# The second block's experts: runs of 1792 columns, a branch on the row count for TensorE, and half of the third matrix unsplit

## Chip, core and metric

One core of one Trainium2 chip. The metric is the device time of one execution in microseconds; TensorE, VectorE (DVE), ScalarE (ACT), GpSimd (POOL) and SyncE (SP, which issues most loads) run side by side and wait for one another by semaphores.

## What is computed

256 tokens of width 1024 pass a first block (latent attention beside a recurrent group, then 32 small experts) and a second block of two layers. The second layer of the second block ends in eight large experts, and that is where the change lies:

```python
def swiglu(h, w1, w3, w2):
    return (jax.nn.silu(h @ w1) * (h @ w3)) @ w2

def moe_swiglu(h, w_router, w1, w3, w2):
    B, S, D = h.shape
    t = h.reshape(B * S, D)
    logits = (t @ w_router).astype(jnp.float32)
    top_vals, top_idx = lax.top_k(logits, TOP_K)
    top_w = jax.nn.softmax(top_vals, axis=-1)
    gates = jnp.sum(jax.nn.one_hot(top_idx, N_EXPERTS_2, dtype=jnp.float32) * top_w[..., None],
                    axis=1).astype(h.dtype)
    out = jnp.zeros_like(t)
    for e in range(N_EXPERTS_2):
        out = out + gates[:, e:e + 1] * swiglu(t, w1[e], w3[e], w2[e])
    return out.reshape(B, S, D)
```

Each token goes to two of the eight experts. `w1` and `w3` of an expert are 1024 x 3584 and `w2` is 3584 x 1024, in fp32: 44 MB per expert, 352 MB in all. After the experts come a layer norm and a gated addition, which end the kernel.

## The kernel before

Products whose operands are wide are made of split operands: `K.split` (line 88) makes `hi`, a copy in the reduced format fp32r by ScalarE, and `lo`, the rest, by VectorE (or GpSimd, if asked), and `K.mm3` (line 110) adds hi x hi, hi x lo and lo x hi on TensorE, three matmuls for one. In line numbers of the profile ScalarE's half of a split is L99, VectorE's is L100, and the three matmuls are L113, L114 and L115.

The experts are in `moe` (line 1514). The router's logits give each token two experts; the rank of a token within its expert is its slot, up to 128 slots. `gather` makes the transposed rows of the slots of two experts at a time, split into `xgh` and `xgl`, by products with one-hot matrices (L1574). An expert then goes through `NS` = 7 steps of 512 hidden columns. In a step `half` makes the 512 gate columns and, called again, the 512 up columns: for each it loads two tiles [128, 4, 512] of 1 MB, splits them, and makes 24 matmuls with the slots' rows as the stationary operand and the weights moving. `hidden` (L1603, L1604) makes silu(gate) x up, `turned` transposes it by four transposes (L1610) and splits it, and `down` loads and splits two tiles of `w2` and adds 24 matmuls to two banks of sums. The second product of a step is issued between the products of the next (`second`, a generator). At an expert's end `finish` splits the sums, puts the rows back to their tokens (`back`, L1631) and adds them into `x` with the routing weights (`add`, L1636).

Weights come by SP's queue (L85) through a ring of 6 tiles (`raw`), and the split halves lie in a ring of 4 (`spl`); both rings stay open through all phases of the second block (`stream_pools` in `whole`). In the experts, two or three of eight loads go to other room (`xgh1`, `xgl1`, `xw`). Instructions of an engine run in the order of the program text, except where `K.behind` (line 103) puts some behind a named instruction. PSUM has eight banks of 512 columns.

`past` (L1684, L1685) is a branch of all engines for experts with more than 128 rows; its body isn't run here. A like branch stands in the first block's experts (L993). Those 32 experts (L1074, L1105) use unsplit fp32 weights with 32 slots each, four experts side by side in four groups of 32 columns of the array.

The tail of `mixer` makes `p @ ple_w` for the first token tile (`ple_products`); in the second layer the second tile's product is made in `moe`, while the routes are made.

## Time and profile before

| | us |
|---|---|
| median of 3 runs | 1985.56 |
| lowest and highest | 1983.2, 1987.6 |
| span of the profiled execution | 1980.7 |
| TensorE busy (matmul) | 1845.0 (93%) |
| VectorE busy | 1402.4 (71%) |
| ScalarE busy | 1102.0 (56%) |
| GpSimd busy | 171.9 (9%) |
| read from memory | 543 MB, 275 GB/s over the span |

The busy times are those of one execution, which spanned 1980.7 us from its first to its last instruction. Matmuls overlap their neighbours' latency, so that a matmul's own duration (some 0.39 us for 512 columns) is longer than the distance at which the next one starts; the price of one in a row is that distance. A group's idle time names who ended most of it.

### The profile page before, as it was taken

To read this page: it belongs to the slowest core of one execution; us is meant where nothing else is said; L and a number is where in the kernel's file an instruction comes from. 1 tells how busy PE (TensorE), PEld (TensorE's weight loads), DVE (VectorE), ACT (ScalarE), POOL (GpSimd) and SP (SyncE) were. 2 spreads that over 40 slices of the span, in tenths; PEclk is the share of its full clock that TensorE was granted. 3 is DMA by queue.
4 is the path that set the end of the run, shared out by engine and by line. 5 is a ranking of instruction groups with operands and counts; after the bars stand their busy time and mean duration, and the time that the engine had idled before them with its cause. 6 is when DMAs were issued, how large, how long until landed. Compare 5 with 4: busy or idle time off the path is not lost. (4 is left out here: it accounts for less than half of the span.)

```text
span 1980.7 us, 25915 instructions
## 1 busy us (share of the span) xinstructions
PE 1845.0 (93%) x10327; PEld 1471.6 (74%) x10327; DVE 1402.4 (71%) x1508; ACT 1102.0 (56%) x1223; POOL 171.9 (9%) x249
## 2 busy tenths in 40 slices
PE   7988698877989999888999999999999999999997
PEld 6878464323779999777888887878878778788785
DVE  5675542101886554887889889888888888888986
ACT  6444341101474443555777666776767666677673
POOL 3051210000400000234100000000000000000002
PEclk8989689989999999999999999999999999999998
DMA  7000579999755555444899889999999999899991
GB/s 223 30 1 1 201 288 402 421 421 401 261 165 178 186 186 174 150 149 161 300 377 367 301 327 346 366 363 356 349 334 363 340 371 343 309 365 374 347 373 53
DMA packets 224412, 545.82 MB, mean 276 GB/s; under 512 B 12817, under 2 KB 45724, under 8 KB 211997
## 3 DMA queue, kind: packets, MB, share of 16 engines
q1 hardware_dynamic: 218476, 536.06, 73.2%
q10 hardware_dynamic: 5536, 6.99, 1.1%
q8 instruction: 83, 1.36, 0.3%
q0 software_dynamic: 272, 1.05, 0.2%
q14 instruction: 45, 0.36, 0.1%
HBM read 543.01 MB, written 1.05 MB: 275 GB/s over the span
## 5 line engine op out<-in xcount | busy, mean ns | idle before, releaser
L100 DVE TENSOR_TENSOR wlo<-raw,whi 128x2048 fp32r<-128x2048 f32 (+1 forms) x436 | 804.7, 1881 | 147.2 <-ACT whi L99 146.7
L99 ACT ACTIVATE whi<-raw 128x2048 fp32r<-128x2048 f32 (+1 forms) x460 | 679.2, 1526 | 102.6 <-PE ps L115 68.6
L114 PE MATMUL ps<-wlo,xgh 128*128 128x512 f32 x896 | 358.3, 400 | 5.0 <-PEq L1685 3.8
L113 PE MATMUL ps<-whi,xgh 128*128 128x512 f32 x896 | 354.9, 396 | 0.0
L115 PE MATMUL ps<-whi,xgl 128*128 128x512 f32 x896 | 351.7, 393 | 0.0
L114 PEld LDWEIGHTS ps<-wlo,xgh 128*128 128x128 f32 x896 | 169.0, 189 | 47.1 <-DVE wlo L100 8.8
L113 PEld LDWEIGHTS ps<-whi,xgh 128*128 128x128 f32 x896 | 168.6, 188 | 38.1
L115 PEld LDWEIGHTS ps<-whi,xgl 128*128 128x128 f32 x896 | 169.1, 189 | 35.4
L114 PE MATMUL ps<-wlo,hTh 128*128 128x512 f32 x452 | 180.1, 399 | 2.0 <-DVE wlo L100 2.0
L115 PE MATMUL ps<-whi,hTl 128*128 128x512 f32 x452 | 177.1, 392 | 0.8 <-DVE hTl L100 0.8
L113 PE MATMUL ps<-whi,hTh 128*128 128x512 f32 x452 | 163.9, 392 | 0.2 <-ACT hTh L99 0.2
L114 PE MATMUL ps<-xTl,whi 128*128 128x256 f32 x576 | 161.9, 282 | 1.5 <-DVE xTl L100 1.5
L115 PE MATMUL ps<-xTh,wlo 128*128 128x256 f32 x544 | 153.8, 284 | 3.0 <-DVE wlo L100 2.8
L113 PE MATMUL ps<-xTh,whi 128*128 128x256 f32 x544 | 152.0, 282 | 0.4 <-ACT xTh L99 0.4
L100 POOL TENSOR_TENSOR wlo<-raw,whi 128x512 fp32r<-128x512 f32 (+2 forms) x24 | 41.5, 1758 | 1072.5 <-PE ps L1631 990.4
L99 ACT ACTIVATE hTh<-ps 128x512 fp32r<-128x512 f32 x56 | 33.5, 598 | 148.7 <-PE ps L1610 145.4
L114 PEld LDWEIGHTS ps<-xTl,whi 128*128 128x128 f32 x576 | 108.7, 189 | 3.6 <-DVE xTl L100 2.6
L115 PEld LDWEIGHTS ps<-xTh,wlo 128*128 128x128 f32 x544 | 104.2, 192 | 5.3 <-DVE wlo L100 5.2
L114 PEld LDWEIGHTS ps<-wlo,hTh 128*128 128x128 f32 x452 | 85.1, 188 | 28.9 <-DVE wlo L100 12.4
L113 PEld LDWEIGHTS ps<-xTh,whi 128*128 128x128 f32 x544 | 102.3, 189 | 1.7 <-ACT xTh L99 0.9
L100 DVE TENSOR_TENSOR wlo<-xw,whi 128x2048 fp32r<-128x2048 f32 (+1 forms) x43 | 96.2, 2236 | 5.0 <-ACT whi L99 5.0
L113 PEld LDWEIGHTS ps<-whi,hTh 128*128 128x128 f32 x452 | 85.2, 188 | 18.6 <-ACT hTh L99 0.5
(526 smaller groups left out, 2749.6 us busy)
## 6 DMA issues: line engine op xcount, KB each, us to landing
raw<-in_exp_w_dram SPq DMA_DIRECT2D x280, 1024.0 KB
xw<-in_exp_w_dram SPq DMA_DIRECT2D x40, 1024.0 KB
raw<-in_dense_w_dram SPq DMA_DIRECT2D x33, 1024.0 KB
gu<-in_w_up_dram SPq DMA_DIRECT2D x32, 1024.0 KB
dn<-in_w_down_dram SPq DMA_DIRECT2D x32, 1024.0 KB
gu<-in_w_gate_dram SPq DMA_DIRECT2D x29, 1024.0 KB
raw<-in_w_in_dram SPq DMA_DIRECT2D x19, 1024.0 KB
raw<-in_w_out_dram SPq DMA_DIRECT2D x8, 1024.0 KB
```

The lines of the kernel that those rows point to most:

```text
L99: self.last = [nc.scalar.activation(hi[o], src[o], AF.Copy).ins, (engine or nc.vector).tensor_tensor(lo[o], src[o], hi[o], op=SUB).ins]
L100: (engine or nc.vector).tensor_tensor(lo[o], src[o], hi[o], op=SUB).ins]
L113: mm(out, a[0], b[0], start=first, stop=False)
L114: mm(out, a[0], b[1], start=False, stop=False)
L115: return mm(out, a[1], b[0], start=False, stop=last).ins
```

## The change

- An expert goes through `NS` = 2 runs of 1792 hidden columns. A tile of `w1` or `w3` is 128 rows x 1792 columns (917,504 bytes, 7 KB per partition in one piece); a run's gate columns stand in four banks (`BANKS`), then its up columns.
- After the last tile of gate or up, ScalarE copies the four banks out to SBUF (`evict`). They are transposed by TensorE unhidden, gate and up both (`turn`), four chunks of 128 at a time into two banks; silu and the product with up are made of the transposed values (`turned`).
- The slots are ordered so that rows 0 to 63 of an expert stand at even places, and `g` holds high and low parts in one tile. A register of TensorE holds each expert's row count (`many`), and `arms` makes a branch: over 64 rows, three products as before; else `piece` takes a stationary operand of 64 high and 64 low columns (every second element of 256) and makes two products, with the weights' high and low parts. The sum of both halves is made in `turn`, by an fp32 product with the matrix `both` in place of a transpose, and at the end through the one-hot matrix (`transposed`). Where `cut` is set a product is made in pieces of 256 columns, so that both arms have as many instructions.
- Of the 14 chunks of a run's part of `w2`, seven are split as before (tiles 0 to 3), and seven (tiles 4 to 7) are used as loaded, in unsplit fp32, for few rows with 64 stationary columns, the two halves of the output in two column groups.
- The loop goes by jobs of two tiles: four of gate, four of up, then four of the run before in `w2`; the next job's loads and splits are issued ahead of a job's products.
- `ple_products` of both token tiles stand in the mixer's tail. The rings are closed before and after the experts; theirs have six tiles raw and four split, of 1792 columns. Two tiles are loaded early to the room of the second pair's rows.

Comments were also taken out. Of the diff, what the text speaks of:

```diff
-EX = 60    # loads of the second block's experts before the first pair's rows have been used
+RAW = 6
...
-        for t in range(1 if l else 2):
+        for t in range(NT):
             self.ple_products(t, tuple(z[:, :, t * P:(t + 1) * P] for z in pT))
...
-        E, NS = 8, 7
+        E, NS, HALF = 8, 2, P // 2
+        MS, R = 1792, 7
+        BANKS = ((0, 512), (512, 512), (1024, 512), (1536, 256))
...
+        up_of = lambda n, e, s, k: a[n][0, e, k * P:(k + 1) * P, s * MS:(s + 1) * MS]
+        def down_of(e, s, j):
+            o = s * MS + j // 4 * (MS // 2)
+            rows = a["exp_w2_2"][0, e, o:o + MS // 2, :].rearrange("(p r) d -> p (r d)", r=R)
+            return rows[:, j % 4 * MS:(j % 4 + 1) * MS]
...
+        def arms(e, f):
+            with tc.If(many[e] > HALF) as c:
+                f(False)
+            with c.Else():
+                f(True)
+        def piece(few, rows, w, i, to, first, last, cut):
+            if few:
+                few_rows = rows.rearrange("p i s -> p (i s)")[:, 0::2]
+                n = i.stop - i.start
+                for o in range(0, n, 256 if cut else n):
+                    m = 256 if cut else n
+                    for q in range(2):
+                        mm(to[:, o:o + m], few_rows, w[q][:, i.start + o:i.start + o + m], start=first and o == 0 and q == 0, stop=last and o + m == n and q == 1)
+            else:
+                for q, (a_, b_) in enumerate(((0, 0), (0, 1), (1, 0))):
+                    mm(to, rows[:, a_], w[b_][:, i], start=first and q == 0, stop=last and q == 2)
+        def up(few, e, g, to, k, w):
+            for b, (o, n) in enumerate(BANKS):
+                piece(few, g[:, k, e % 2], w, slice(o, o + n), to[b][:, :n], k == 0, k == KC - 1, b < 2)
+        def down(few, s, hT, acc, j, w):
+            c0, c, cuts = j % 4 * MS, j % 4 * MS, 0
+            while c < c0 + MS:
+                c1 = min((c // 512 + 1) * 512, c0 + MS)
+                r, h = divmod(c // 512, 2)
+                i, to = slice(c - c0, c1 - c0), acc[h][:, c % 512:c % 512 + c1 - c]
+                if j < 4:
+                    cut = c1 - c == 512 and cuts < 2
+                    cuts += cut
+                    piece(few, hT[0][:, r], w, i, to, s == 0 and r == 0, s == NS - 1 and r == R - 1, cut)
+                else:
+                    o = slice(h * HALF, h * HALF + HALF) if few else slice(0, P)
+                    mm(to[o], hT[1][:, R + r, ::2 if few else 1], w[0][:, i], start=False, stop=False)
+                c = c1
+        def turn(few, rows, pt, c0):
+            for c in range(c0, min(c0 + 4, 2 * R)):
+                z = rows[:, c // R * (MS // 2) + c % R:(c // R + 1) * (MS // 2):R]
+                if few:
+                    mm(pt[:, (c - c0) * P:(c - c0 + 1) * P], z, both, start=True, stop=True)
+                else:
+                    nc.tensor.transpose(pt[:, (c - c0) * P:(c - c0 + 1) * P], z, K.ident)
...
+        def take(n, e, s, k, **how):
+            if n == "down":
+                w = K.load(down_of(e, s, k), 1, MS)
+                return k, [z[:, 0] for z in (K.split(w) if k < 4 else (w,))]
+            w = early.get((n, e, s, k))
+            if w is None:
+                w = K.load(up_of(n, e, s, k), 1, MS)
+            hl = K.split(w.rearrange("p k (b q) -> p (k b) q", b=4), **how)
+            return k, [z.rearrange("p b q -> p (b q)") for z in hl]
+        jobs = []
+        for i in range(E * NS + 1):
+            e, s = divmod(i, NS)
+            if i < E * NS:
+                jobs += [(n, e, s, q) for n in ("exp_w1_2", "exp_w3_2") for q in range(0, KC, 2)]
+            if i:
+                jobs += [("down", *divmod(i - 1, NS), q) for q in ((0, 2, 4, 6), (4, 6, 0, 2))[(i - 1) % NS]]
+        taken = {}
+        def ahead(n):
+            if n < len(jobs) and n not in taken:
+                name, e, s, q = jobs[n]
+                taken[n] = [take(name, e, s, q + i) for i in range(2)]
...
+        many = [nc.values_load(cnti[0:1, e:e + 1], engines=[mybir.EngineType.PE], min_val=0, max_val=TOK,
+                               skip_runtime_bounds_check_because="counts of the rows, 0 to 256, made above") for e in range(E)]
...
+            sg = self.W([P, 512], "sg", bufs=1)
+            nc.scalar.activation(sg[:, :n], pts[0][:, :n], AF.Silu)
+            nc.vector.tensor_tensor(hd[:, o], sg[:, :n], pts[1][:, :n], op=MUL)
+            m = min(n, R * P - c * P)
+            if m > 0:
+                o = slice(c, c + m // P)
+                K.split(hT[i][1][:, o], hi=hl[:, o, 0], lo=hl[:, o, 1])
...
+        def evict(banks, tag):
+            z = self.W([P, MS], tag, F32, 1)
+            for b, (o, n) in enumerate(BANKS):
+                nc.scalar.activation(z[:, o:o + n], banks[b][:, :n], AF.Copy)
+            return z
...
+        for n, (name, e, s, q) in enumerate(jobs):
+            ahead(n + 1)
+            i = NS * e + s
+            tiles = taken.pop(n)
+            if name == "down":
+                if s == 0 and q == 0:
+                    accs[e] = [K.ps() for _ in range(2)]
+                if i == E * NS - 1 and q == 4:
+                    for c in range(0, 2 * R, 4):
+                        pts = [K.ps() for _ in range(2)]
+                        arms(e, lambda few: [turn(few, rows, pt, c) for rows, pt in zip(ups[i], pts)])
+                        turned(i, c, pts)
+                arms(e, lambda few: [down(few, s, hT[i], accs[e], *t) for t in tiles])
+                if s == NS - 1 and q == 6:
+                    hotT = transposed(e, gs[e // 2][1])
+                if s == NS - 1 and q == 2:
+                    if e == E - 1:
+                        finish_last(e, accs.pop(e), hotT)
+                    else:
+                        ends = finish(e, accs.pop(e), hotT)
+                        next(ends)
+                continue
+            first = name == "exp_w1_2"
+            if (e, s, q, first) == (E - 2, 1, 0, True):
                 past()
+            if q == 0:
+                banks = [K.ps() for _ in range(4)]
             g = gs[e // 2][0]
+            before = first and i > 0
+            if before:
+                pts = [K.ps() for _ in range(2)]
+            if before and NS * ((i - 1) // NS) != NS * e:
+                arms(e, lambda few: [up(few, e, g, banks, *t) for t in tiles])
+                arms((i - 1) // NS, lambda few: [turn(few, rows, pt, 2 * q) for rows, pt in zip(ups[i - 1], pts)])
+            else:
+                def f(few):
+                    up(few, e, g, banks, *tiles[0])
+                    if before:
+                        for rows, pt in zip(ups[i - 1], pts):
+                            turn(few, rows, pt, 2 * q)
+                    up(few, e, g, banks, *tiles[1])
+                arms(e, f)
+            if before:
+                turned(i - 1, 2 * q, pts)
+            if q == 6:
+                z = evict(banks, "gs" if first else "us")
+                ups.setdefault(i, []).append(z)
+                if not first and e % 2 and s == NS - 1 and e + 1 < E:
+                    gs[e // 2 + 1] = pair_of(e + 1, hots(e + 1))
+            if first and q in (2, 6):
+                next(ends, None)
...
+            with ExitStack() as c3:
+                K.stream_pools(c3, 6, 4)
+                B.phase("mix0", B.mixer, 0)
+                B.phase("ffn", B.dense)
+                B.phase("ple0", B.ple, 0)
+                B.phase("mix1", B.mixer, 1)
+            with ExitStack() as c3:
+                K.stream_pools(c3, RAW, 4)
+                B.phase("moe", B.moe)
+            with ExitStack() as c3:
+                K.stream_pools(c3, 6, 4)
+                B.phase("ple1", B.ple, 1, out)
```

## Rows read from the trace of the kernel before

**Rows 1.** Stretches: from:to us, length, busy us (instructions) by engine, clock, DMA share, GB/s.

```profile
300.00:380.00 80.00, 65.66 (x406) 28.80 (x404) 13.49 (x37) 8.33 (x16) 0.00 (x0) 0.95 1.01 421
...
1200.00:1300.00 100.00, 99.59 (x447) 80.64 (x446) 87.77 (x52) 72.37 (x50) 0.00 (x0) 1.00 0.97 353
```

**Rows 2.** First products (instructions by tile, first and last start) and the last one (timeline).

```profile
L113 PE MATMUL ps<-whi,xgh x896: 387/392/628, 943.7 to 1925.5; 128*128 128x512 f32 x180
...
1939.20 0.39 PE L115 MATMUL ps<-whi,hTl 128*128 128x512 f32 x1
```

**Rows 3.** Waits of SP's queue, 960 to 1940: waited in total, times, longest.

```profile
SPq L85 <- DVE wlo L100: 798.6, 276, 11.5
```

**Rows 4.** Timeline (start us, us, engine, line, operation) of the experts' products, 1600 to 1611.

```profile
1600.34 0.40 PE L113 MATMUL ps<-whi,xgh 128*128 128x512 f32 x1
...
1604.05 0.39 PE L114 MATMUL ps<-wlo,xgh 128*128 128x512 f32 x1
...
1610.29 0.60 PE L1610 MATMUL ps<-t,hd 128*128 128x128 f32 x4
...
1610.65 0.48 PE L114 MATMUL ps<-wlo,xgh 128*128 128x512 f32 x1
```

**Rows 5.** Timeline of 256-column products in the dense layer, first and last of 31.

```profile
699.80 0.28 PE L115 MATMUL ps<-xTh,wlo 128*128 128x256 f32 x1
...
703.33 0.28 PE L115 MATMUL ps<-xTh,wlo 128*128 128x256 f32 x1
```

**Rows 6.** Unsplit fp32 products: a group by line (count | busy, mean ns), then timeline.

```profile
L1074 PE MATMUL ps<-gu,xg 128*32 128x512 f32 x464 | 61.6, 594 | 0.0
...
139.81 1.50 PE L634 MATMUL ps<-t,Hl 128*128 128x128 f32 x12
...
485.60 6.61 PE L1074 MATMUL ps<-gu,xg 128*32 128x512 f32 x58
...
547.49 1.89 PE L1357 MATMUL ps<-pd,cbtl 128*128 128x256 f32 x8
```

**Rows 7.** Branches of past() (ns, start us), one of the first block; timeline around it.

```profile
L993 PEldq COMPARE_BRANCH  x1: 2125/2125/2125, 489.4 to 489.4; - x1
...
L1685 SPq COMPARE_BRANCH  x1: 53/53/53, 1676.7 to 1676.7; - x1
...
L1685 SPq EVENT_SEMAPHORE  x1: 17/17/17, 1676.9 to 1676.9; - x1
...
L1685 PEldq COMPARE_BRANCH  x1: 6003/6003/6003, 1686.7 to 1686.7; - x1
...
1688.82 0.39 PE L113 MATMUL ps<-whi,xgh 128*128 128x512 f32 x1
...
1692.98 0.77 PE L114 MATMUL ps<-wlo,xgh 128*128 128x512 f32 x1 [3.77 <-PEq L1685]
...
1696.04 0.40 PE L115 MATMUL ps<-whi,xgl 128*128 128x512 f32 x1
```

**Rows 8.** Groups by line, 1000 to 1900: count | busy us, mean ns | idle before, releaser.

```profile
L100 DVE TENSOR_TENSOR wlo<-raw,whi 128x2048 fp32r<-128x2048 f32 x255 | 575.4, 2287 | 64.0 <-ACT whi L99 63.5 <-DVEq L1685 0.3
...
L99 ACT ACTIVATE whi<-raw 128x2048 fp32r<-128x2048 f32 x256 | 477.7, 1912 | 37.8 <-PE ps L115 37.8
...
L1604 DVE TENSOR_TENSOR hd<-sg,ps 128x512 f32<-128x512 f32 x51 | 35.0, 686 | 33.4 <-PE ps L115 33.4
...
L1603 ACT ACTIVATE sg<-ps 128x512 f32<-128x512 f32 x50 | 29.9, 597 | 49.0 <-PE ps L115 49.0
```

**Rows 9.** Transfers of two stretches, 1100 to 1900 and 250 to 500.

```profile
DMA packets 117710, 280.07 MB, mean 350 GB/s; under 512 B 4256, under 2 KB 4256, under 8 KB 117665
...
DMA packets 13953, 96.21 MB, mean 385 GB/s; under 512 B 1470, under 2 KB 1470, under 8 KB 2472
```

**Rows 10.** Timeline of TensorE at the end of the second layer's mixer.

```profile
923.44 1.39 PE L1207 MATMUL ps<-t,t 128*128 128x128 f32 x8 [2.30 <-DVE t L1271]
```

More of the change, by code (lines that the diff above doesn't have):

```diff
@@ L1666, in transposed, with back, add, ended @@
             return hotT
+        def back(d, hotT, t, ps):
+            for i in range(2):
+                mm(ps, hotT[:, t, :], d[i], start=(i == 0), stop=(i == 1))
+            return ps
+        def add(e, ps, t, h):
+            o = x[:, t, h * 512:(h + 1) * 512]
+            nc.vector.scalar_tensor_tensor(o, ps, comb[:, t, e:e + 1], o, op0=MUL, op1=ADD)
+        def ended(acc, h, bufs=1):
+            return K.split(acc[h], hi=self.W([P, 512], "dh", F32R, 1), lo=self.W([P, 512], "dl", F32R, 1))
+        def finish(e, acc, hotT):
+            for h in range(2):
+                d = ended(acc, h)
+                yield
+                ps = [back(d, hotT, t, K.ps()) for t in range(NT)]
+                for t in range(NT):
+                    add(e, ps[t], t, h)
+            yield
+        def finish_last(e, acc, hotT):
+            z = self.W([P, MS], "gs", F32R, 1)
+            ds = [ended(acc, 0), K.split(acc[1], hi=z[:, :512], lo=z[:, 512:1024])]
+            K.warm(AF.Sqrt, ds[1][0][:, 0:1].bitcast(F32))
+            ps = [[back(ds[h], hotT, t, K.ps()) for h in range(2)] for t in range(NT)]
+            self.xT = self.pair()
+            gb = self.W([P, 2 * KC * TOK], "xg0", F32, 1)
+            for t in self.norm(None, "ln2_g_2", "ln2_b_2", 1, after=[K.loaded], gb=[gb[:, :D], gb[:, D:2 * D]]):
+                if t == 1:
+                    self.rows_T(self.xT, (0,))
+                if t < NT:
+                    with K.behind(K.applied if t else None):
+                        for h in range(2):
+                            add(e, ps[t][h], t, h)
         def hots(e):
@@ L1754, in past @@
                         nc.vector.tensor_copy(ci[:, 0:E - 1], s3[:, 1:E])
-        rest = iter(())
         h = hots(0)
-        first = []
-        for n in ("exp_w1_2", "exp_w3_2"):
-            for q in range(2):
-                with K.behind(rows + self.hot if first[1:] else None):
-                    first.append(K.split(load(half_of(n, 0, 0, q), 4, 512), parts=PARTS,
-                                         engine=None if len(first) == 2 else nc.gpsimd))
-        with K.behind(beside):
-            gs = {0: pair_of(0, h)}
+        nc.vector.tensor_copy(cnti, cnt)
+        def take(n, e, s, k, **how):
[19 more added lines that the diff above has]
+                taken[n] = [take(name, e, s, q + i) for i in range(2)]
+        for n in range(2):
+            name, e, s, q = jobs[n]
+            taken[n] = []
+            for i in range(2):
+                with K.behind(rows + self.hot if n or i else None):
+                    taken[n].append(take(name, e, s, q + i, parts=PARTS, engine=None if (n, i) == (1, 0) else nc.gpsimd))
+        gs = {0: pair_of(0, h)}
         for t in range(NT):
@@ L1777, in moe @@
         nc.vector.tensor_copy(mosti, most)
-        nc.vector.tensor_copy(cnti, cnt)
-        accs = {}
-        def second(e, s, hd):
-            hT = turned(hd)
-            if s == NS - 1:
-                hotT = transposed(lambda t: gs[e // 2][1][:, t, e % 2, :])
-            yield
-            if s == 0:
-                accs[e] = [K.ps() for _ in range(2)]
-            down(e, hT, accs[e], s, e == E - 1 and s == NS - 1)
-            if s == NS - 1:
-                ends[0] = finish(accs[e], hotT, lambda t: comb[:, t, e:e + 1], e == E - 1)
-                next(ends[0], None)
-            yield
@@ L1808, in moe @@
-            next(rest, None)
-            rest = second(e, s, hd)
-        for _ in rest:
-            pass
+            before = first and i > 0
[12 more added lines that the diff above has]
+                arms(e, f)
```

171 lines of the change are left out of this document (42 added, 129 removed).

## The prediction

> **What bounds the kernel now.** I read the stretches first [rows 1]. [...] The experts' products run from 943.7 to 1939.6 us [rows 2], 995 us or half of the profiled span of 1980.7. The rest of the kernel hardly changes, so only this stretch is costed. [...]
>
> Unit prices come next. A split matmul of 512 columns starts 0.232 us after the one before (16 intervals from 1600.34 to 1604.05); four transposes take 0.36 us [rows 4]. One of 256 columns takes 0.118 (30 intervals from 699.80 to 703.33) [rows 5], so cutting a product in two costs nothing, and a column costs 0.453 ns however it is cut. An unsplit fp32 product leaves two records: line 1074 issues 232 of them at 512 columns and shows 464 [rows 6]. At 256 columns eight records take 1.89 us, the last being 0.38 of latency: 0.216 each, 0.43 per product, 0.864 for 512 columns. At 128x128 it is (1.50 - 0.275) / 11 x 2 = 0.223 us. In line 1074 four experts sit in four column groups of 32, and 58 records take 6.61 us; four products of 512 columns (eight records) thus cost 0.91 us, about one alone: column groups run side by side.
>
> **The stage before, as a check.** An expert has 504 split matmuls and 28 transposes: 504 x 0.232 + 28 x 0.09 = 119.4 us, eight 955. The other 40 us are what stays: the skipped branch of past(), 5 us [rows 7], and 4.4 us per expert of gathers, rows put back and waits.
>
> **TensorE after, by expert.** Run on the reference's seeded inputs, the router gives the eight experts 100, 119, 57, 49, 70, 27, 48 and 42 rows: three take the long arm (over 64), five the short one. Nothing in the trace shows these counts.
> - Long arm: 32 tiles of 1792 columns x 3 products = 77.9 us; the split half of the third matrix, 2 x 7 x 1024 x 3 columns, 19.5; the unsplit half, 28 products at 0.864, 24.2 (before: 19.5); transposes of both gate and up, 56 x 0.09 = 5.0. Sum 126.6.
> - Short arm: two products for three, 52.0 and 13.0; the unsplit half as pairs in two column groups of 64, 14 x 0.864 = 12.1; 56 fp32 turns at 0.223 = 12.5. Sum 89.6. No row has groups of 64: the ends are 12.1 (paired, as the groups of 32 are) and 24.2 (not). I take 12.1, the nearest row.
>
> **What is new around them.** Four banks of gate or up are now copied out by ScalarE (0.597 us for 512 columns, from the row of line 1603 [rows 8]: 2.2 us a set). Eight banks hold four outputs, two turned and two sums, so the up products wait for the gate's banks once a run. Ends: 0 (the turned pair's two free banks cover it) and 2.4 (all four copies and a hand-over). I take half, 1.2, or 2.4 per expert. With the 4.4 that stay: long 133.4, short 96.4.
>
> **The other limits per expert.** Transfers: 48 tiles of 917,504 bytes. The rate comes from the first block's experts, whose runs are 8 KB: 421 GB/s over 80 us [rows 1], at 6.9 KB per packet, against 2.4 KB and 350 GB/s now [rows 9]. The new runs are 7 KB, so 421: 104.6 us. VectorE: a tile of 1792 costs 2287 x 1792/2048 = 2.0 us; 40 of them (8 of 48 are no longer split) 80, with 2 x 3.5 hidden products at 0.686, some halves and the 8 us of sums and gathers, 96. ScalarE: 40 x 1.67 + 9 for evictions + 7 = 83. All of these lie beside TensorE. So a long expert costs 133.4 (TensorE) and a short one 104.6 (transfers); I add 2.4 us to the short one, since the six loads of the ring can't bridge each bank wait.
>
> **Edits at nothing.** The second token tile's product with ple_w moves into the mixer's end: TensorE waits there 2.30 us for the norm [rows 10], and 2.8 us of products go beside it; without that cover, 2.8. [...] Eight counts are loaded to TensorE, its queue alone, some 3 us. The rings are closed and opened around the stage, which may delay the first loads behind SP's queue. I book 2 us for these together, ends -2 and 8.
>
> **Branches.** There are 232 pairs of arms, all on TensorE's queue: 128 for up and gate, 28 extra where a run's turn belongs to the expert before, 68 for the third matrix and its last turn, 8 for the transposed marks. Queued behind each are the next tile's matmuls; ScalarE and VectorE wait for those to free places. Rows bound the price: SP's branch over an empty body costs 0.2 us to its next instruction; TensorE's two branches over long bodies took 2.1 and 6.0 us, and the second left it idle 3.77 us, after which seven matmuls took 3.06 us, half speed, until the clock rose [rows 7]. But TensorE still had 2.2 us queued when that branch began (1686.7 against 1688.82). The new jumps pass some 50 to 80 instructions, so SP's row is the nearest, and 0.2 us hides behind 2.2 us of queued work. I take 0.
>
> [...]
>
> **Sum.** 3 x 133.4 + 5 x 107.0 + 5 + 2 = 942 us against 995: -53. The span becomes 1928, and the median lies 4.9 us above the profiled span, so **1933 us**. With every hand-over hidden (131 and 100 per expert) the stage takes 898 and the time is 1889; with unpaired groups and full bank waits (138 and 114) it takes 991 and the time is 1982. That is the forecast's own range.
>
> **Rivals.**
> - **Exposed branches (slower).** If TensorE's queue runs dry at each arm, 29 branches per expert add to a long one at once and to a short one only past the 10.6 us between 107.0 and 96.4. The gain of 53 is gone at 3 x 29c + 5 x (29c - 10.6) = 53, c = 0.46 us. Halfway between SP's 0.2 and TensorE's 2.1, c = 1.1: 96 + 107 = 203 more, about 2136. Were each to fetch at 2.1, 183 + 252: about 2370. For it: both rows of TensorE are above 2 us, and DMA traffic is denser now. Against: those bodies are hundreds of instructions long.
> - **Strided weight loads (slower).** The short arm loads every second element, the turn every seventh; no row has such a load. If it took twice the 0.09 us that bounds a plain one (the transposes), the 256-column pieces would go at 0.18: 10 per tile x 0.062 x 32, plus 6 in the third matrix, 26 us per short expert, 122 against 107: 78 more, 2011. Against: nothing in the rows either way.
> - **Transfers stay at their present rate.** The stage moves 340 to 363 GB/s with the engines over 0.9. At 360 a short expert costs 122.3 + 2.4: 88 more, 2021. Against it stands the 421 of the first block's experts. [...]
> - **The split does not happen.** If the branches went by other counts and all eight took the long arm, 8 x 133.4 + 7 = 1074: 2065.
>
> **How the numbers follow.** Forecast 0.63; exposed branches 0.17, with a fetch each another 0.03; strided loads 0.08; transfers 0.07; no split 0.02. The range 1886 to 2070 takes in the forecast's own range and the cheaper rivals, and leaves out the dearer half of the branches and a little below. About 0.2%, 4 us, is what a measurement can tell from no change. Faster 0.63, with 0.04 for a small change out of the upper end and the cheap branches, slower 0.33.
>
> **What would show it.** In the trace after: products of 256 columns start 0.118 apart in the short experts, three of eight experts about 133 us long and five about 107; the DMA rate in a short expert near 420; TensorE idle there by transfers or splits, not by its own queue; COMPARE_BRANCH on TensorE near 0.1 us with no idle behind it; two fp32 records of different banks overlapping. Idle put down to TensorE's queue, or a short expert above 115 us, would make the forecast wrong.

## The result and the profile after

The changed kernel takes **2020.8 us** where the kernel before takes 1984.4: a ratio of 1.018, 95% interval 1.0164 to 1.0197, so it is 36 us slower. Forecast were 1933 us and a gain. The profiled execution of the changed kernel has a span of 2020.8 us as well.

Ends of the stage, from the instructions by line and the timeline of TensorE: the first up product and the last product of the third matrix.

```profile
L1607 PE MATMUL ps<-whi,xg x768: 274/392/792, 949.0 to 1547.0; 128*128 128x512 f32 x192
...
1971.92 0.39 PE L1604 MATMUL ps<-wlo,hT 128*128 128x512 f32 x1
```

The experts' products now run from 949.0 to 1972 us, 1023 us, against 995 before [rows 2]. The stage begins 5 us later than before, and from its last product to the end of the span it is 48.5 us where it was 41.1. By the sum of the prediction the stage should have taken 942 and the span 1928. So 81 of the 93 us that are missing lie between the first and the last product, 5 ahead of them and 7 behind.

Where inside? The last copy of an up matrix out of PSUM (line 1846, `us`) marks the end of each run's up products, and from one expert's mark to the next is what an expert costs. The eighth expert, a short one behind a short one, takes 122 us (1804.8 to 1926.9); the short experts before it 122 to 129, where each has some of a neighbour's work in it; 107 were forecast. The long ones fit the forecast of 133.4: in after the two that can be read from mark to mark take 138.4 and 129.8, and the kernel e3_all_long below, in which all are long, has 133.8 as the mean of its second to eighth. The five short experts take 627 us from mark to mark where 535 were forecast: the miss of the stage is in them.

Three stretches, the last being the eighth expert, in the columns of [rows 1]:

```profile
1200.00:1300.00 100.00, 95.69 (x541) 81.44 (x543) 77.93 (x57) 66.84 (x60) 0.00 (x0) 1.00 0.94 357
1300.00:1400.00 100.00, 92.50 (x534) 80.07 (x530) 73.74 (x53) 65.84 (x59) 0.00 (x0) 1.00 0.94 364
1804.00:1927.00 123.00, 114.91 (x681) 99.63 (x680) 91.97 (x63) 81.04 (x73) 0.00 (x0) 1.00 0.95 368
```

In a short expert TensorE was to be idle a good tenth of the time, waiting for transfers at 420 GB/s. It is busy 115 of 123 us instead, VectorE has fallen to 75%, and the transfers run at 368 GB/s. TensorE has more to do than the sum gave it. The groups by line, 1000 to 1900 us, say what (count | busy us, mean ns of one | idle before):

```profile
L1635 PE MATMUL ps<-t,gs 128*128 128x128 f32 x248 | 62.9, 394 | 0.0
L1635 PE MATMUL ps<-t,us 128*128 128x128 f32 x240 | 61.2, 395 | 0.0
L1635 PEld LDWEIGHTS ps<-t,gs 128*128 128x128 f32 x248 | 60.2, 325 | 0.0
...
L1604 PEld LDWEIGHTS ps<-whi,xg 128*128 128x128 f32 x894 | 176.8, 198 | 26.2 <-issue 12.5 <-ACT gs L1846 4.1 <-ACT whi L99 2.1
...
L1607 PEld LDWEIGHTS ps<-whi,xg 128*128 128x128 f32 x608 | 111.5, 188 | 22.1 <-ACT whi L99 0.8 <-issue 0.6 <-ACT gs L1846 0.4
```

A turn of the short arm (line 1635) loads every seventh column of the copied-out rows as weights, and such a load takes 325 ns. A load of every second column (line 1604, the short arm's products) takes 198, a plain one (line 1607) 188. The timeline in the eighth expert shows what that makes of the turns: two groups of eight records, of which the first takes 1.85 us until the next group starts and the second 1.77.

```profile
1822.60 2.02 PE L1635 MATMUL ps<-t,gs 128*128 128x128 f32 x8
1824.45 2.02 PE L1635 MATMUL ps<-t,us 128*128 128x128 f32 x8
1826.22 0.37 PE L1604 MATMUL ps<-whi,xg 128*128 128x256 f32 x1
```

Within all such groups a record starts 0.232 us after the one before (median), 0.46 a turn; the sum had 0.223 a turn. The products of 256 columns start 0.120 us apart, as forecast.

**Theory A**, with which the experiments began: the stride of the turns' weight loads is the cause; 56 turns at 0.46 instead of 0.223 are 13 us per short expert, 64 in all. **Rivals**: transfers set the pace whatever TensorE does (the forecast's rival of 2021 us gives nearly the measured time); the 319 branches cost time after all; the unsplit half of the third matrix holds places of the load ring and leaves VectorE idle (theory D below).

### The profile page after: what moved, and what is told of

It is laid out like the page before. It is cut to its first block, busy times and chain, and to the rows that moved or that the text cites. A ratio compares the mean times of both kernels' runs of the same rounds, so it can differ in the third digit from the quotient of the medians.

```text
span 2020.8 us, 28225 instructions
## 1 busy us (share of the span) xinstructions
PE 1827.3 (90%) x11151; PEld 1476.8 (73%) x11151; DVE 1275.5 (63%) x1491; ACT 1056.0 (52%) x1318; POOL 169.8 (8%) x251
## 5 line engine op out<-in xcount | busy, mean ns | idle before, releaser
L100 DVE TENSOR_TENSOR wlo<-raw,whi 128x1792 fp32r<-128x1792 f32 (+2 forms) x474 | 810.2, 1738 | 289.1 <-ACT whi L99 286.3
L99 ACT ACTIVATE whi<-raw 128x1792 fp32r<-128x1792 f32 (+3 forms) x498 | 691.4, 1423 | 252.6 <-DMA raw<-in_exp_w_dram 126.6
L1604 PE MATMUL ps<-whi,xg 128*128 128x256 f32 (+1 forms) x960 | 268.1, 310 | 13.6 <-issue 9.9
L1604 PE MATMUL ps<-wlo,xg 128*128 128x256 f32 (+1 forms) x960 | 265.6, 307 | 16.3 <-DVE wlo L100 16.2
L1607 PE MATMUL ps<-whi,xg 128*128 128x512 f32 (+1 forms) x768 | 223.1, 369 | 0.0
L1604 PEld LDWEIGHTS ps<-wlo,xg 128*128 128x128 f32 x960 | 189.1, 197 | 31.8 <-DVE wlo L100 24.9
L1604 PEld LDWEIGHTS ps<-whi,xg 128*128 128x128 f32 x960 | 189.7, 198 | 26.7 <-issue 12.5
L1607 PEld LDWEIGHTS ps<-whi,xg 128*128 128x128 f32 x768 | 140.4, 188 | 27.5 <-ACT whi L99 0.8
L1607 PE MATMUL ps<-wlo,xg 128*128 128x512 f32 (+1 forms) x384 | 140.9, 367 | 1.2 <-DVE wlo L100 1.2
L1627 PE MATMUL ps<-raw,hd 128*64 128x512 f32 (+3 forms) x512 | 140.0, 554 | 1.4 <-DVE hd L1837 1.4
L1105 PE MATMUL ps<-dn,hT 128*32 128x512 f32 x256 | 70.3, 662 | 19.5 <-DMA dn<-in_w_down_dram 19.5
L1607 PEld LDWEIGHTS ps<-wlo,xg 128*128 128x128 f32 x384 | 72.3, 188 | 15.5 <-DVE wlo L100 2.3
```

The source lines that it names most:

```text
L99: self.last = [nc.scalar.activation(hi[o], src[o], AF.Copy).ins, (engine or nc.vector).tensor_tensor(lo[o], src[o], hi[o], op=SUB).ins]
L100: (engine or nc.vector).tensor_tensor(lo[o], src[o], hi[o], op=SUB).ins]
L1105: nc.tensor.matmul(ps[32 * e:32 * e + 32, :], hT[:, k, 32 * e:32 * e + 32], wd[e][:, k, hs], start=(k == 0), stop=(k == 1))
L1604: mm(to[:, o:o + m], few_rows, w[q][:, i.start + o:i.start + o + m], start=first and o == 0 and q == 0, stop=last and o + m == n and q == 1)
L1607: mm(to, rows[:, a_], w[b_][:, i], start=first and q == 0, stop=last and q == 2)
L1627: mm(to[o], hT[1][:, R + r, ::2 if few else 1], w[0][:, i], start=False, stop=False)
```

## The experiments

Ratios are to the kernel before, measured beside each; it came out between 1983.8 and 1986.8 us there. Where two kernels are compared below, the difference is that of their times; taken from the ratios it is up to 4 us smaller or larger.

### e1: the turns' columns put side by side

```diff
-        BANKS = ((0, 512), (512, 512), (1024, 512), (1536, 256))
+        BANKS = ((0, 448), (448, 448), (896, 448), (1344, 448))
...
-                    m = 256 if cut else n
+                    m = min(256, n - o) if cut else n
...
-                z = rows[:, c // R * (MS // 2) + c % R:(c // R + 1) * (MS // 2):R]
+                z = rows[:, c * P:(c + 1) * P]
...
-                nc.scalar.activation(z[:, o:o + n], banks[b][:, :n], AF.Copy)
+                to = z.rearrange("p (h r t q) -> p h r t q", h=2, r=R, t=2)[:, b // 2, :, b % 2, :]
+                nc.scalar.activation(to, banks[b][:, :n].rearrange("p (q r) -> p r q", r=R), AF.Copy)
```

> The gate and up rows are copied out of PSUM in four pieces of 448 columns, already in the order in which the turns read them, so that each turn loads 128 neighbouring columns as its weights instead of every seventh; nothing else is changed. Theory A (the stride makes a turn's weight load slow): the records of the short arm's turns start 0.11 us apart instead of 0.232, LDWEIGHTS of the turns 0.19 us instead of 0.326, 12.8 us of TensorE per short expert gone; if TensorE is the bound there, 5 x 8 to 5 x 13 us less, 1955 to 1981. Rival B (the short experts wait for transfers): the turns get cheaper as in A, TensorE idles instead, and the time stays within 5 us of 2021. Rival C (a turn costs what it costs because of its 128 fp32 columns, not of the stride): records stay 0.23 apart, 2021.

1985.7 us, ratio 1.0006 (0.9997 to 1.0016): 35 us less than after, level with before. The records of the turns start 0.112 apart, so A's mechanism is there, but the gain is a little under its range. This edit brought a cost of its own: the short arm cuts two of its four pieces, now into 256 and 192 columns each, and these eight products of a tile take 1.02 us (median of the seventh and eighth expert), 0.127 each, where their columns would allow 0.81. Behind a product of 192 columns the next starts 0.09 us later within a pair and 0.11 to 0.12 behind it (timeline of TensorE):

```profile
1854.22 0.28 PE L1604 MATMUL ps<-wlo,xg 128*128 128x256 f32 x1
1854.34 0.25 PE L1604 MATMUL ps<-whi,xg 128*128 128x192 f32 x1
1854.43 0.28 PE L1604 MATMUL ps<-wlo,xg 128*128 128x192 f32 x1
1854.54 0.31 PE L1604 MATMUL ps<-whi,xg 128*128 128x256 f32 x1
```

### e13: the turn's columns alone

To part the stride from the pieces, this one changes the turn's line only. The line serves both arms, so the long arm's transposes load neighbouring columns too.

```diff
-                z = rows[:, c // R * (MS // 2) + c % R:(c // R + 1) * (MS // 2):R]
+                z = rows[:, c * P:(c + 1) * P]
```

> After, and only the turns changed: each loads 128 neighbouring columns as its weights instead of every seventh; the copies out of PSUM and the pieces (512, 512, 512, 256) stay. The rows of the third matrix then meet other hidden values than they should; the work is the same in number and size. e1_contig changed the pieces as well, whose 192-column products cost 7 us per short expert. If the stride of the turns' weight loads is the cause: turns 0.112 us apart, and without e1's new cost the time falls below e1's 1986, to 1962 to 1980. If half of e1's gain came from the pieces or the copies: about 2000.

1970.2 us, ratio 0.9926 (0.9909 to 0.9943): **51 us less** than after, and below the kernel before. One line of stride decides the sign of the whole change. The groups and the timeline of this kernel, to be held against those of after:

```profile
L1635 PE MATMUL ps<-t,gs 128*128 128x128 f32 x280 | 38.9, 280 | 1.5 <-DVE hd L1837 1.5
...
L1635 PEld LDWEIGHTS ps<-t,gs 128*128 128x128 f32 x280 | 35.4, 195 | 3.1 <-PE ps L1604 2.2 <-issue 0.8
```

```profile
1842.54 1.05 PE L1635 MATMUL ps<-t,gs 128*128 128x128 f32 x8
1843.43 1.06 PE L1635 MATMUL ps<-t,us 128*128 128x128 f32 x8
```

Its eighth expert, in the columns of [rows 1]:

```profile
1770.60:1882.50 111.90, 102.51 (x670) 86.30 (x670) 90.68 (x63) 80.29 (x71) 0.00 (x0) 0.98 1.00 397
```

Eight records take 0.89 us instead of 1.85; a load takes 195 ns instead of 325. The eighth expert falls from 122 to 112 us. Of the 64 us that TensorE is spared in the short arms, and 2.5 in the long ones (168 transposes at 0.109 instead of 0.124), 51 arrive at the end. The rest does not show in the time: other limits come next (e8 and e17).

### e14: the cut alone

```diff
-                piece(few, g[:, k, e % 2], w, slice(o, o + n), to[b][:, :n], k == 0, k == KC - 1, b < 2)
+                piece(few, g[:, k, e % 2], w, slice(o, o + n), to[b][:, :n], k == 0, k == KC - 1, False)
...
-                    cut = c1 - c == 512 and cuts < 2
+                    cut = False
```

> After, with the short arm's two cut pieces left whole (512 columns in one product instead of 256 and 256); turns as in after. In after products of 256 columns start 0.120 us apart, those of 512 0.233: the cut should cost under 0.01 us each, 1 us per expert. Within 5 us of 2021. If fewer weight loads matter in themselves (the loads of every second column take longer than a plain one): 5 x 3 to 5 x 7 us less, 1986 to 2006.

2014.6 us, ratio 1.0154 (1.0137 to 1.0171): 6 us less than after, about the edge of "free". Cutting 512 into two of 256 costs next to nothing, as forecast; cutting 448 costs more (next).

### e5: both

e1 and e14 together.

> e1_contig, and the short arm no longer cuts two of its four pieces (448 columns in one product instead of 256 and 192; in the third matrix 512 instead of 256 and 256). In e1_contig the pieces of 192 columns started 0.116 us after one another, as those of 256 do in after (0.120), while 448 took 0.205: the short arm's weight loads (every second column) seem to need about 0.115 us each. Theory A (that load is a floor, and TensorE still sets the pace of the short experts): 7 us of TensorE less per short expert, 5 x 4 to 5 x 7 us, 1951 to 1966. Rival B (with the turns mended the short experts go by their transfers): TensorE waits instead, 1978 to 1990. Rival C (0.116 is no floor, the pieces only waited): 1986.

1967.4 us, ratio 0.9903 (0.9886 to 0.9919), 18 less than e1: a microsecond above A's range, and both rivals fall. The short arm's products thus need about 0.12 us each, with 192 columns (0.127 in e1) as with 256 (0.120); at 256 columns this costs next to nothing. That the load of every second column sets this floor is not shown: in the kernel before, 64-column products behind side-by-side weights (line 634, 178.7 to 180.5 us) start 0.112 us apart as well, like those of 128 columns there.

### e8 and e17: are transfers the pace?

In the up matrix, e8 leaves out every second load and splits the tile before a second time; e17 leaves out the load and its split and uses the split tiles before twice. The rest is e5. First e8's edit, then e17's.

```diff
-                w = K.load(up_of(n, e, s, k), 1, MS)
+                if n == "exp_w3_2" and k % 2:
+                    w = held[0]
+                else:
+                    w = held[0] = K.load(up_of(n, e, s, k), 1, MS)
```

```diff
+            if n == "exp_w3_2" and k % 2:
+                return k, held[0]
...
-            return k, [z.rearrange("p b q -> p (b q)") for z in hl]
+            held[0] = [z.rearrange("p b q -> p (b q)") for z in hl]
+            return k, held[0]
```

> e5_contig_uncut, where the odd blocks of 128 rows of the up matrix (exp_w3) are not loaded: the even block's tile is split a second time in their place. A sixth of the experts' bytes is left out (and with it the right values); products, splits and copies are as many as in e5. If transfers set the pace of the short experts there: 5 x 5 to 5 x 10 us less than e5. If TensorE or the splits do: within 5 us of e5.

1969.2 us, ratio 0.9911 (0.9894 to 0.9927): nothing is gained, though in the eighth expert the DMA share is down to 0.86 and the rate to 326 GB/s:

```profile
1765.60:1878.80 113.20, 104.40 (x507) 82.86 (x507) 89.19 (x62) 78.75 (x72) 0.00 (x0) 0.95 0.86 326
```

Loads alone are not what holds the short experts.

> e5_contig_uncut, where the odd blocks of 128 rows of the up matrix (exp_w3) are neither loaded nor split: the even block's split tiles are used twice. A sixth of the experts' bytes and a fifth of their splits are left out (and the right values with them); TensorE's products, turns and copies are as many as in e5. e8_fewer_loads left out the same loads alone and gained nothing. If transfers and splits hold the short experts together, each close to TensorE's own 96 us: 5 x 8 to 5 x 14 us less than e5's 1967, 1897 to 1927. If TensorE's own hand-overs (banks, turned values) hold them: within 10 us of 1967.

1934.6 us, ratio 0.9746 (0.9729 to 0.9762): 33 less than e5, short of the 40 to 70 expected but far from the rival's none. The eighth expert over its length in e5 and in e17:

```profile
1764.00:1876.00 112.00, 103.40 (x511) 82.30 (x510) 90.79 (x62) 80.57 (x74) 0.00 (x0) 0.97 1.00 399
```

```profile
1746.00:1850.00 104.00, 99.06 (x508) 81.45 (x507) 73.95 (x53) 66.11 (x63) 0.00 (x0) 0.98 0.93 355
```

In e5 the DMA engines are busy all the time at 399 GB/s, TensorE has 92% and VectorE 81%, and lifting one of the three (e8) leaves the pace to the others. In e17 TensorE is at 95%, with its waits for VectorE's halves cut (weight loads: 12.8 us in e5's eighth expert, 4.4 here), and the expert is at 104 us, still 8 above the 96 that the sum gave TensorE alone. A kernel with all loads and fewer splits was not run. Against the splits as the only limit stands e12 below: eight tiles more to split per expert, and an eighth expert of 110 us.

### e2, e16 and e6: the branches

In e2 (on after) and e16 (on e12, below) the arm is chosen when the kernel is built; e6 puts a second branch into after's short arm.

```diff
-            with tc.If(many[e] > HALF) as c:
-                f(False)
-            with c.Else():
-                f(True)
+            f((100, 119, 57, 49, 70, 27, 48, 42)[e] <= HALF)
```

```diff
             with c.Else():
-                f(True)
+                with tc.If(many[e] > 0) as c2:
+                    f(True)
```

> Each expert's arm is chosen when the kernel is built, by the counts of these inputs (long for experts 0, 1 and 4, short for the others); the branches on the row count are left out, all else is as after. If a branch costs nothing beside queued work: within 6 us of 2021 (the one of 5.0 us behind the skipped body of past() may go). If each of the 319 taken or passed branches holds TensorE up for its median of 0.2 us: 64 us less, 1957. Half exposed: 1990.

> e12_all_split_contig with the arms chosen when the kernel is built (no branch on the row count). If the 319 branches cost what TensorE's own queue shows as idle (under 12 us in all): 1941 to 1953. If removing them changes the order in which the splits and copies are queued, as it may have in e2_fixed_arms (12 us slower): 1955 to 1970. If each branch cost its 0.2 us: 1890.

> After, with a second branch on the row count (always taken the same way for the short experts) inside the short arm: twice the branches there, some 145 more in all, nothing else. If a branch is hidden behind the products that TensorE has queued: within 5 us of 2021. If each costs its 0.2 us: 2050. If about half are exposed: 2035.

e2 takes 2032.8 us (1.0243, 1.0226 to 1.026), 12 **more** than with branches; e16 takes 1974.0 (0.994, 0.9922 to 0.9958), 21 more than e12; e6 takes 2096.5 (1.055, 1.0514 to 1.0585), 76 more than after. None of the three fits a price per branch. Without branches the time should not rise, and in e6 it rises before a second branch has run: the first of its 290 records starts at 1199.1 us, but the second expert's mark comes at 1183.5 us where after has 1170.1, 13 us later, with the first products at 949 us in both. The waits of TensorE and of its weight loads at the short arm's products (line 1604) in after, then in e6 (line 1605; us in total, times, longest):

```profile
PE ps L1604 <- DVE wlo L100: 27.2, 42, 1.7
...
PEld ps L1604 <- DVE wlo L100: 40.7, 63, 1.9
PEld ps L1604 <- issue: 18.6, 13, 10.2
```

```profile
PE ps L1605 <- DVE wlo L100: 56.2, 60, 2.4
...
PEld ps L1605 <- DVE wlo L100: 77.7, 101, 2.7
PEld ps L1605 <- issue: 13.2, 8, 9.3
```

Twice the branches leave TensorE's wait for its own queue ("issue") where it was, 18.6 and 13.2 us, of which 10.2 and 9.3 are the one long stall at past(). What doubles is the wait for split tiles. And e2 runs its turns in another order: in the eighth expert after has groups of 8 and 8 records between two tiles, e2 groups of 8 and 6, of 2 and 8. VectorE's queue differs too: from 930 us on, e13 has the same 610 instructions, by operation and tile, in the same order as after, e2 and e6 do not. So taking branches out or putting them in also changes the order in which work is queued; if that is the cause, the order is worth 12 to 76 us here. That it is the cause of all three is argued from these rows, not shown: no kernel was run in which the order stayed and the branches went.

### e7 and e15: the test for rows past the cap

```diff
-            if (e, s, q, first) == (E - 2, 1, 0, True):
-                past()
```

> After without the test for rows past the cap (and so without its skipped body; with these inputs no expert has more than 128 rows, so nothing computed is lost). In after, TensorE's branch over that body took 5.8 us, and the next arm's branch, 6 us later, another 5.0. If both stand on the path: 8 to 12 us less, 2009 to 2013. If only the first does, as in the kernel before: 5 us less, 2016. If other work covers both: 2021.

2011.4 us, ratio 1.0125 (1.0107 to 1.0142): 9 us less than after, so both long branches are on the path. The branches by line (count, shortest/median/longest in ns), then TensorE's timeline:

```profile
L1590 PEldq COMPARE_BRANCH  x319: 65/202/4973, 946.8 to 1966.2; - x160
...
L1707 PEldq COMPARE_BRANCH  x1: 5821/5821/5821, 1720.5 to 1720.5; - x1
```

```profile
1721.44 0.38 PE L1646 MATMUL ps<-t,sg 128*128 128x128 f32 x2
1731.74 0.58 PE L1604 MATMUL ps<-whi,xg 128*128 128x256 f32 x1 [9.92 <-issue]
1732.11 0.42 PE L1604 MATMUL ps<-wlo,xg 128*128 128x256 f32 x1
1732.33 0.41 PE L1604 MATMUL ps<-whi,xg 128*128 128x256 f32 x1
```

The branch over the body of past() takes 5.8 us, and the next arm's branch, the one of 4973 ns, comes right behind it. In the time of each the queue of instructions (q8) moves one packet of 16 KB, between 1723.5 and 1724 us and between 1728.5 and 1729.5, of 132 in the run; that the branch waits for it was not shown. TensorE is idle for 9.92 us (3.77 before [rows 7]); then its products of 256 columns start 0.21 us apart, at a granted clock of 0.50, until about 1736, from where it is 1.00. The second long branch is not always there: in e5 and e12 the arm's branch behind past() is a short one, and TensorE is idle for 5.7 and 5.0 us.

e15 (on e12) moves the call behind the last up product.

> e12_all_split_contig with the test for rows past the cap moved from the middle of the seventh expert to behind the last up product, where TensorE has gaps (in after it stands idle for some 10 us there, waiting for hidden values and loads). If the two fetches of 5 to 6 us each hide there: 5 to 9 us less than e12_all_split_contig's 1953. If that stretch is one chain: no less, or up to 5 us more.

1963.6 us, ratio 0.9893 (0.987 to 0.9917): 10 **more** than e12. From the last copy of up to the last product of the third matrix it is 54.7 us instead of 42.5, and the seventh expert gets back 4 (110.4 for 114.1). TensorE is idle for 5.3 us behind the branch, and from 1861 to 1882 its granted clock is 0.71 and 0.62, where e12 has 1.00 in the like place. So the gaps there hide nothing of it; that they are one chain of turns, hidden values and products is argued.

### e3: what the short arm is worth

> No branches, and all eight experts take the long arm (three products per piece, transposes, unsplit half at full rows). The long experts of after take some 131 us each, the short ones 122 to 129. Theory A (the short arm saves little, since its turns and waits take back what two products for three save): 5 x 2 to 5 x 9 us more, 2031 to 2066. If the short arm were worth what was forecast (26 us per expert): 2150.

2059.8 us, ratio 1.0384 (1.0361 to 1.0407), 27 more than e2, which has no branches either: as the short arm stands in after, it saves 5 us per short expert (8 if e3 is held against after) where 26 were forecast. The forecast's rival "the split does not happen" had put eight long arms at 2065.

### e4: a deeper load ring

```diff
-RAW = 6
+RAW = 8
...
-                K.stream_pools(c3, RAW, 4)
+                K.stream_pools(c3, RAW, 3)
```

> The ring of loads has eight places instead of six, paid for by three pairs of split tiles instead of four; nothing else is changed. If the loads are held up by unsplit tiles that keep places of the ring (SP waited 11 to 27 us per short expert for the unsplit products), the DMA rate in a short expert rises from 341-361 GB/s and the time falls by 10 to 30 us, 1991 to 2011. If TensorE's own work is the bound: within 5 us of 2021. If the split ring was the tighter one: slower, 2026 to 2050.

2027.0 us, ratio 1.021 (1.0193 to 1.0227), 6 more than after. More room for loads paid by less for split tiles gains nothing. A deeper ring by itself was not tried.

### e11 and e12: the third matrix split throughout

e11 undoes the third part of the change on after, e12 does it on e5: all fourteen chunks go through split products, and VectorE and ScalarE split eight tiles more per expert. Of the edit, the line of the loads:

```diff
...
-                return k, [z[:, 0] for z in (K.split(w) if k < 4 else (w,))]
+                return k, [z[:, 0] for z in K.split(w)]
...
```

> After with the third part of the change undone: the second half of the third matrix is split as well and takes split products (three or two per piece) instead of fp32 ones; turns, cuts and order as in after. TensorE: 4.7 us less per long expert, 0.9 more per short one; VectorE and ScalarE: eight tiles more per expert, 16 and 14 us. Theory D (the unsplit block leaves VectorE idle and starves the next stretch): the idle goes, the extra splits fill it, 1990 to 2015. Rival V (VectorE's work sets the pace): 5 x 8 us more, 2030 to 2060.

> e5_contig_uncut with the whole third matrix split, as in e11_all_split. Its short experts would have 112 us of VectorE against 113 us measured in e5, its long ones 4.7 us less of TensorE. Theory D: 1945 to 1970. Rival V: 1985 to 2010.

e11 takes 2004.0 us (1.0099, 1.0082 to 1.0115), 17 less than after; e12 **1953.1 us** (0.9851, 0.9834 to 0.9867), 14 less than e5 (10 by the ratios) and the best kernel here that does all of the work. So the unsplit half was a loss of 10 to 17 us. The sum's own prices give 3 x 4.7 us for the long experts less 5 x 0.9 for the short ones, 10 in all, but the place doesn't fit: the seventh and eighth expert, short ones behind short ones, take 123.9 and 118.6 us in e11 where after has 128.1 and 122.1, some 4 less each. Why is not settled. In e12 they are level with e5 (114.1 and 110.3 for 113.5 and 111.1), so the extra splits cost nothing visible there, though VectorE is then close to full, as this stretch of e12 shows:

```profile
1700.00:1800.00 100.00, 92.60 (x468) 77.93 (x469) 97.27 (x69) 85.02 (x74) 0.00 (x0) 1.00 1.00 395
```

### e9 and e10: unsplit products dealt out

Theory D rests on stretches like these two of e5: in an unsplit block VectorE and ScalarE do next to nothing, among the up products VectorE is full.

```profile
1820.00:1825.00 5.00, 5.00 (x30) 2.33 (x26) 0.00 (x0) 1.08 (x1) 0.00 (x0) 1.00 1.01 420
...
1865.00:1870.00 5.00, 4.87 (x21) 3.98 (x22) 5.00 (x4) 4.37 (x3) 0.00 (x0) 1.00 0.99 376
```

```diff
+            downs = [("down", *divmod(i - 1, NS), q) for q in ((0, 4, 2, 6), (4, 0, 6, 2))[(i - 1) % NS]] if i else []
...
-                jobs += [("down", *divmod(i - 1, NS), q) for q in ((0, 2, 4, 6), (4, 6, 0, 2))[(i - 1) % NS]]
...
+                for q in range(0, KC, 2):
+                    jobs += [("exp_w3_2", e, s, q)] + downs[q // 2:q // 2 + 1]
```

e10 is e9 with this:

```diff
-parts=PARTS, engine=nc.gpsimd) for h in range(2)}
+parts=PARTS, engine=None if h else nc.gpsimd) for h in range(2)}
```

> e5_contig_uncut, with the products of the third matrix dealt out between the up products of the next run (one split or unsplit pair behind each pair of the second up matrix, split and unsplit in turn) instead of all four pairs after them. Theory D (the unsplit half needs no splitting, so VectorE and ScalarE stand idle while its 6 us of products run in a block, and in the up stretch VectorE is busy throughout and TensorE waits for it; with room for only four split tiles the two phases don't even out): 5 to 9 us less per short expert, 1922 to 1942. Rival T (transfers set the pace, 104.6 us per expert at 421 GB/s): 1955 to 1967. Rival P (the order of the queues gets worse): slower than 1967.

> e9_interleaved, and half of the first eight splits of the last gate matrix go to VectorE instead of GpSimd. In after TensorE waited for GpSimd's eight subtractions (10.7 us from 1986.5) where ScalarE's half took 4.3. If that chain is on the path: 3 to 6 us less than e9_interleaved. If not: the same.

e9 takes 1985.9 us (1.001, 0.9998 to 1.0021), 18 more than e5; e10 1987.0 (1.0019, 1.0008 to 1.003). D's forecast falls: the eighth expert stays at 112 us, with a DMA share of 0.99 and 388 to 393 GB/s in its last two short experts, so the transfers have no room left there, and the second, fourth and fifth expert take 6 to 10 us more than in e5. Nor is GpSimd's share of the last gate's splits on the path.

## Why the prediction was wrong, point by point

**The step that failed** is the term of the short arm "56 fp32 turns at 0.223 = 12.5". The row under it, twelve records at 128x128 in 1.50 us [rows 6], has weights side by side; the turn loads every seventh column, and there it is 0.46 a turn, 25.3 us per expert (the starts of the seventh's and eighth's records summed). Of the 64 us in five experts e13 gives 51 back. Without the stride the change is faster than before.

That price alone would not have given the measured time. By the sum's own rule, that an expert costs the larger of TensorE's work and its transfers, it makes a short expert 109.2 us instead of 107.0, and the forecast 1944. After's eighth expert takes 122 us, and 112 with the turn mended. So **the rule of the larger one failed too**: the limits add to each other in part, which the sum had covered with 2.4 us per expert. How they do so is argued from e8 and e17, not shown.

The rival **strided weight loads** had the mechanism and a chance of 0.08, but the price in the wrong place: it doubled the loads of every second column under the 256-column products (26 us per expert) and left the turns at their plain price. It is the other way round: 0.120 for those products, 0.232 for the turn's records. The prediction said itself that no row has such a load, and still gave the turn one price without bounds.

What the stride costs a weight load the trace gives: 198 ns at every second column and 325 at every seventh, against 188 side by side; why the seventh costs so much more was not shown. The size depends on more than the stride: the long arm's transposes load the same every seventh column in 211 to 216 ns instead of 140 (e13), and start 0.124 us apart instead of 0.109. Why the turn loses so much more is open.

**Transfers stay at their present rate** came to 2021 and so to the measured time, for another reason. With all bytes loaded, e13 gains 51 us, and with a sixth of them left out, e8 gains none. The rate of 368 GB/s in after followed from TensorE's pace: with the turns mended it is 397 in the same expert (e13). The forecast of 107 us by 421 GB/s was still too good: mended short experts behind a short one take 111 to 118 (e5). That is the size of the second error, some 5 x 4 to 5 x 11 us. The sum took the largest of three limits that lie within a tenth of each other (104.6, 96.4 and 96 us) as the time, with 2.4 us for all hand-overs; e8 and e17 show that it is not the transfers alone that hold the pace.

**Branches** at nothing: the 319 records of line 1590 have a median of 0.2 us, and the idle that the weight loads of the short arm's products put down to their own queue is 18.6 us, 10.2 of it at one place. That each would fetch at 2.1 us, to which the forecast gave 0.03, no run shows: of the 241 from 1000 to 1720 us the longest takes 0.36. The one place, past(), was booked at its old 5 us; it costs 9 (e7), with a second long branch right behind the first. What changed branches do to the order of the queues (e2, e6, e16) the prediction didn't ask.

**What held.** Long experts 133.8 (e3) for 133.4; 2022 ns for a split of 1792 columns (2.0); the copies out of PSUM 595 ns (0.597). The unsplit products do run side by side in two column groups of 64. The same 32 records, 24 of 512 columns and 8 of 256, take 12.19 us in the long arm and 6.29 in the short one (timeline):

```profile
1605.98 12.19 PE L1627 MATMUL ps<-raw,hd 128*128 128x512 f32 x32
```

```profile
1941.15 6.29 PE L1627 MATMUL ps<-raw,hd 128*64 128x512 f32 x32
```

**Edits at nothing** were booked at 2 us, ends -2 and 8; 13 us have appeared at the stage's two ends. The 5 ahead of it change from kernel to kernel (the first product starts between 944.5 and 950.3 in those above). The 7 behind it stay, at 47 to 49 us in all of them where before has 41: the last gate's loads are issued here, once the experts' ring is closed (queue of SP), while before they went out at 1917, 22 us ahead of the last product.

```profile
1969.48 2.17 SPq L85 DMA_DIRECT2D raw<-in_ple_gate_w_dram  x4
```

That this is why was not tried.

**Range and sign.** 1886 to 2070 holds 2020.8, through its rivals. The chance of 0.63 for faster stood on a sum whose one new kind of operand had been priced by a row of another kind. The sign of its own that the prediction named, a short expert above 115 us, is what came.

## What to carry to other kernels

Price an operation by a row with the same access pattern, not only the same shape; where none exists, give both ends to every place that uses the pattern, the small ones too. When several limits lie close together, an experiment that lifts one may show nothing (e8); lift two, and don't take the largest as the time. When an edit adds or removes blocks of control flow, look at the order of every engine's queue before putting the difference down to the branch.

## What the runs showed of the hardware

- Weight loads in fp32, 128x128: 188 ns side by side (195 for the turn's own in e13), 198 at every second column, 325 at every seventh. With the last, the turn's products of 128 columns start 0.232 us apart instead of 0.112; the long arm's transposes with the same stride 0.124 instead of 0.109 (e13).
- ScalarE reads PSUM at every seventh column without a visible loss: 448 columns took 545 to 549 ns in e1, between the 595 for 512 and the 400 for 256 of after, on the line through both.
- Runs of 7168 bytes reach 420 GB/s over 5 us (e5) and 399 over 112 us.
